# A new list for the even mixer in quarter slices, an earlier first input, earlier bank release and a later spread of the norm's factors in a two-layer encoder trunk

## The chip, the core and the metric

The kernel runs on one core of one Trainium2 chip. The time is the device time of one execution in microseconds (us). Before the change it is 1195.79 us, the median of 3 runs (1194.28 to 1196.98). The core has five engines with a queue of instructions each: PE (matmuls), DVE (vector), ACT (scalar), POOL (GpSimd) and SP, which issues nearly all of the DMAs.

## The reference, cut to what matters

The input is one sequence of 256 tokens of 1024 numbers. Two layers follow one another; each has a SwiGLU feed-forward part (FFN), a mixer, and a second FFN. The mixer of layer 0 ("even") runs attention and a recurrence (RWKV-7) side by side, that of layer 1 ("odd") is a retention.

```
x = x + 0.5 * rms_norm(swiglu(rms_norm(x, g[0]), w_gu, w_d), g[1])
h = rms_norm(x, g[2])
z = h @ w_in                                 # even mixer: q, k, v of attention; r, k, v, low of RWKV-7
oa = rms_norm(diff_attention(qa, ka, va, lam), subln) * (1 - lam_init)
ob = group_norm(rwkv7_recurrence(r, decay, k, v, kk, a)) + bonus, times the gate
x = x + rms_norm(concat(oa, ob) @ w_out, g[3])
x = x + 0.5 * rms_norm(swiglu(rms_norm(x, g[4]), w_gu, w_d), g[5])
```

swiglu(x) is (silu(x W_gate) * (x W_up)) W_down with an inner width of 2816. The recurrence's token shift mixes each token's value with that of the token before it.

## The kernel before

**Tiling.** The 256 tokens are two blocks of 128, b0 and b1 (in the tables x_75 and x_76). All products keep fp32 accuracy by splitting each operand in two parts, a high one (xh, wh) and a rest (xl, wl). A weight tile `raw` (128x1024, 512 KB) is loaded by SP, ACT casts it to `wh` (L307), DVE subtracts to get `wl` (L308). `pump` issues the loads in the order of use and at most so far ahead as there are buffers. A projection of 512 columns is 24 matmuls on two units of weights (L327 to L329), an output product 12 for each unit (L341 to L343), a projection with the weights held still 48 of 256 columns (L354 to L356). The FFN's 11 chunks of 256 inner columns are done for each block apart ("solo") or for both blocks at once ("joint", L370 and L371); JOINT says which. The first FFN has chunk 0 solo, the other three have chunks 0 and 1 solo.

**Norms.** `pre` transposes a block on PE (L434) and writes xp on ACT and DVE (L439, L440). The norm's factor `rs` of a row is a sum of squares on ACT (L421), a sum on DVE (L413) and a power on POOL (L416). Solo chunks take it as a scalar; joint chunks need it along the free axis, so `spread` copies it on DVE to `rw` (L454), transposes that on PE (L456) and copies the result to `rsb` on ACT (L457). `post` (L468 to L487) adds a block's result: two sums of squares on ACT, two products on DVE, a power on POOL, and two updates of x (L487).

**The even mixer.** Its PE order is written by a small planner: a stream of the units in EVEN_ORDER (the two blocks in turn), cut in slices, and between the slices the steps of jobs (feature, low, value, the recurrence's `core`, attention) by their rank, as soon as an estimated clock has reached the time that each step's `yield` gives. The other engines' order follows from priorities. For each block and for each of two groups of 256 columns, `rwkv_features` makes decays (pc L1074, w L1077, L1078), `kk` (L1082), and on POOL the product `fr` (L1095); the sums `pn` (L1109 on kk, L1110 on fr) follow. Then come pl (L1157), px (L1164) and a chain of small products p (L1175, L1181) with DVE steps between. Value (L833 to L840) moves z one token down by DMAs that POOL issues, since b1's first row comes from b0. At the end of the core comes the group norm (L1313 to L1325), and `mr`; attention ends with hx (L1047); four output units of each block follow, first those of attention.

**Buffers.** `t2` is one pool of five tiles for all short-lived rows of 512: z, zs, mu, kk, low, rw, yg, sgh and others.

Of the kernel before, what the change touches and what calls it, by code (L numbers as in the profile page):

```python
# [17 lines left out]
P = 128  # L18
# [10 lines left out]

NRAW0, FIRST = 12, 56  # L30
CONSTANTS = 40
LAG = 3
LAG0 = (6, 12)
WIDE = 16
LIFT_PRE, LIFT_POST = 300, 100
X = (0, 1, 2)
SPLIT = 6
# [6 lines left out]

EVEN_ORDER = ("k", "r", "low", "q2", "k2", "v", "v2")
PLAN = [("ffn", 0, 0), ("even", 0, 0), ("ffn", 0, 1), ("ffn", 1, 0), ("odd", 1, 0), ("ffn", 1, 1)]
# [59 lines left out]
def _layout(inputs):  # L106
# [23 lines left out]
    def even():  # L130
        w, out = a["even_w_in"][0], []
        b0 = 1536
        at = {"k": b0 + 512, "r": b0, "v": b0 + 1024, "q2": 0, "k2": 512, "v2": 1024}
        for c in EVEN_ORDER:
            if c == "low":
                out += list(cols(w[:, b0 + 1536 :], 8))
            elif c in ("q2", "k2"):
                out += [cols(w[:, i : i + 256], 8)[0] for i in (at[c], at[c] + 256)]
            else:
                out += list(cols(w[:, at[c] : at[c] + 512]))  # L140
        return out + list(cols(a["even_w_out"][0], 2))

# [70 lines left out]
class Trunk:  # L213
    def __init__(self, ctx, tc, io, out, plan):
        self.tc, self.nc, self.io, self.out, self.plan = tc, tc.nc, io, out, plan
        nc = self.nc
        pool = lambda *a, **k: ctx.enter_context(tc.tile_pool(*a, **k))
        self.sb = pool(name="sb", bufs=1)
        self.raw_p = pool(name="raw", bufs=NRAW)
        self.w_p = pool(name="wsp", bufs=NW)  # L220
        self.ps_p = pool(name="ps", bufs=2, space=PSUM)
        self.mix = None
        self.even_cm = tc.tile_pool(name="even", bufs=1)
        self.even_p = self.even_cm.__enter__()
        self.first_cm = tc.tile_pool(name="first", bufs=NRAW0)
        self.first_p = self.first_cm.__enter__()

        c0 = self.sb.tile([P, P + PR_N], F32, name="c0")
        self.ident, self.par = c0[:, :P], c0[:, P:]
        self.mhalf = self.sb.tile([P, 8], F32, name="mhalf")  # L230
        self.x = [self.sb.tile([P, D], F32, name=f"x{b}") for b in range(2)]
        nc.sync.dma_start(out=c0, in_=io["c0"])

        self.ahead = {X[0]: [(0, 0)], X[1]: [(0, 1)], X[2]: [(1, 0), (1, 1)]}
        nc.vector.memset(self.mhalf, -0.5)

# [45 lines left out]
    def pump(self):  # L282
# [3 lines left out]
        while self.n_split < lim:  # L286
            while self.n_dma < min(2 * self.n_units, self.n_split + (NRAW0 if self.n_dma < FIRST else NRAW)):
                i = self.n_dma
                for b, q in self.ahead.pop(i, ()):
                    c = slice(q * 512, q * 512 + 512)  # L290
                    nc.sync.dma_start(out=self.x[b][:, c], in_=self.io["x"][b * P : (b + 1) * P, c])
                r = (self.first_p if i < FIRST else self.raw_p).tile([P, 1024], F32, tag="raw", name="raw")
                self.tc.keep_in_program_order(
# [23 lines left out]
    def proj_slices(self, ps, u, first, last, xT, width=512):  # L317
# [5 lines left out]
        for i in range(n):  # L323
# [5 lines left out]
            mm(ps[:, :width], lhsT=xl[:, kt, :], rhs=h[:, c], start=False, stop=last and i == n - 1)  # L329
            if i == n // 2 - 1:  # L330
                yield "slice", 1.4

# [12 lines left out]
    def features_slices(self, ps, u):  # L345
# [3 lines left out]
        for t in range(2):  # L349
            o = ps[:, t * 256 : t * 256 + 256]  # L350
            for kt in range(8):
                h, l = w[kt // 4]
                c = slice(kt % 4 * 256 + t * P, kt % 4 * 256 + t * P + P)
                mm(o, lhsT=h[:, c], rhs=xh[:, kt], start=kt == 0, stop=False)  # L354
                mm(o, lhsT=h[:, c], rhs=xl[:, kt], start=False, stop=False)
                mm(o, lhsT=l[:, c], rhs=xh[:, kt], start=False, stop=kt == 7)  # L356
                if kt == 3 or (kt == 7 and not t):
                    yield "slice", 1.4

# [132 lines left out]
    def ffn(self, b, u, l, j):  # L492
# [14 lines left out]
        for c in range(NCH + 1):  # L507
            if c == 3:
                self.gpost(gi)
            if c < NCH and not c0 <= c < c1:  # L510
# [11 lines left out]
                u += 1  # L522
                if c0 < c1 and b not in J:
                    self.spread(b, rs)
                    J[b] = True
                t = self.t2("sgh")
                sg, h[c] = t[:, :256], t[:, 256:]
                nc.scalar.activation(out=sg, in_=ps[:, :256], func=AF.Silu, scale=rs[:, 0:1])
                nc.vector.tensor_tensor(out=h[c], in0=ps[:, 256:], in1=sg, op=ALU.mult)
                yield  # L530
# [171 lines left out]
    def even(self, b, u, l, j):  # L702
# [57 lines left out]
        def feature(ps, name, mu, om_at):  # L760
            z = scaled(ps, T2("z"))
            yield 0, 1.3
            yield from self.room(2.6)
            tp = transposes(z, 4)
# [107 lines left out]
        for c in EVEN_ORDER:  # L872
            if c in ("q2", "k2"):
                for i in range(2):
                    if b == 0:
                        ps = self.ps("mm")
                        yield from self.features_slices(ps, u)
                        (queries if c == "q2" else keys)(i, ps)
                        self.stream_took = 1.4
                    else:  # L880
                        self.stream_took = 0
                    u += 1
                    if i and c == "k2":
                        att = self.spawn(1 + 3 * b, self.attention(b, S[f"qT{b}"], kT, rs), 1.5)
                    yield
                continue
            ps = self.ps("mm")
            if c != "low":
                yield from self.proj_slices(ps, u, True, False, xT)
                self.stream_took = 1.4  # L890
                u += 1
# [6 lines left out]
            else:  # L898
                yield from self.proj_slices(ps, u, True, True, xT, 256)
            self.stream_took = 1.4  # L900
            u += 1
            if c in jobs:
                job = self.spawn(2 * b, jobs[c](ps))
                if c == "low":
# [12 lines left out]
        acc = None  # L917
        for i, job in enumerate((att, att, core, core)):
            while not job["done"] or self.now < job["at"] or (acc is None and not free()):
                yield "wait"  # L920
            if acc is None:
                acc = [self.ps(("mm", "ac1")[b]) for _ in range(2)]
            self.outp(acc, u, S.pop(f"{'mr' if i > 1 else 'att'}{b}{i % 2}"), i == 0, i == 3)
            self.stream_took = 2.8
# [50 lines left out]
    def attention(self, b, qT, kT, rs):  # L975
# [6 lines left out]
        ss = self.small(4, "ss4", 2)  # L982
        ma = self.hx(b).bitcast(F32).rearrange("p (a t) -> p a t", a=4)
        for h0 in range(0, 4, H):
            heads = range(h0, h0 + H)
# [28 lines left out]
            for i in range(H):  # L1014
# [4 lines left out]
                )  # L1019
            yield 1.7, 8.0  # L1020
            while f"av{b}" not in S or "pT" in S:
# [25 lines left out]
        V.tensor_tensor(out=ma, in0=ma, in1=r4[:, :, None].to_broadcast([P, 4, P]), op=ALU.mult)  # L1047
        yield 0, 5.0
        for i in range(2):
# [328 lines left out]
    def run(self):  # L1378
# [28 lines left out]

        sizes = {"low": 1, "out": 4}
        turns, at = [], next(at for at, kind in bounds.items() if kind == "even")
        for c in EVEN_ORDER + ("out",):  # L1410
            n = sizes.get(c, 2)
# [76 lines left out]
```

## Time and profile before

| | |
|---|---|
| median of 3 runs | 1195.79 us |
| lowest and highest | 1194.28, 1196.98 us |
| the profiled execution | 1200.61 us, of which its span is 1198.8 us |
| busy in the span | PE 96%, DVE 62%, ACT 52%, POOL 4% |
| granted PE clock, mean | 0.986 of full speed |

One execution was recorded. Its rows give start times from the start of the span. An instruction's row shows in square brackets how long its engine had stood idle before it and what ended that. The durations of matmuls overlap (each is longer than the time to the next), so the pitch from start to start is what a matmul costs. The granted clock is the share of full speed that PE had in a stretch. The profiled execution is 4.82 us longer than the median.

### The profile page before, as it was taken

Reading aid. Unit: us, or ns where it says so; the run is one execution under the profiler, and the core shown is the slowest. Engines: PE = TensorE matmul, PEld = TensorE weight load, DVE = VectorE, ACT = ScalarE, POOL = GpSimd, SP = SyncE. Lnnn points to the kernel's source line nnn. Section 1 sums busy time; section 2 is a strip of 40 time slices with the busy share of each in tenths; the row PEclk is TensorE's granted clock in tenths of the full one; section 3 lists DMA queues with packets and bytes.
Section 4 is the critical chain, followed back from the end, with each engine's and each line's share of the span. In section 5 each row is a group of like instructions: output and inputs, shape, how many; then the busy total and the mean of one; then the engine's idle time right before and its main releaser. Section 6 shows DMA issues by size and latency. Waiting matters only on the chain.

```text
span 1198.8 us, 18578 instructions
## 1 busy us (share of the span) xinstructions
PE 1152.4 (96%) x7314; PEld 955.5 (80%) x7314; DVE 744.8 (62%) x1124; ACT 626.2 (52%) x1054; POOL 51.7 (4%) x79
## 2 busy tenths in 40 slices
PE   6999999999999799999999999999999999999997
PEld 5888887788778687888878888877877777888886
DVE  6665667667663656656676666675545557566664
ACT  7554456763242555555565555575434456555552
POOL 0000000012120100000010000010000001000000
PEclk9999999999999899999999999999999999999999
DMA  9766245432320346555646555556534554656551
GB/s 361 278 209 198 89 134 184 144 120 85 115 89 1 122 149 220 179 190 179 206 138 214 195 182 175 194 188 210 176 98 160 172 168 158 209 184 189 191 192 37
DMA packets 55657, 200.26 MB, mean 167 GB/s; under 512 B 6289, under 2 KB 6545, under 8 KB 55569
## 3 DMA queue, kind: packets, MB, share of 16 engines
q1 hardware_dynamic: 54576, 196.45, 49.2%
q0 software_dynamic: 704, 2.10, 0.6%
q8 instruction: 57, 0.93, 0.3%
q10 hardware_dynamic: 288, 0.52, 0.1%
q14 instruction: 32, 0.25, 0.1%
HBM read 197.47 MB, written 1.05 MB: 166 GB/s over the span
## 4 chain that ended last, share of the span: by engine, by line
PE 77%; DMA 8%; DVE 7%; ACT 4%; issue 2%; POOL 1%; SPq 0%; DVEq 0%; POOLq 0%; ACTq 0%
PE ps L370 22%; PE ps L371 11%; PE ps L341 7%; PE ps L343 7%; PE ps L342 7%; DMA raw<-in_wts_dram 7%; PE ps L327 5%; PE ps L329 4%; PE ps L328 4%; DVE wl L308 3%; ACT wh L307 2%; PE yp L619 1%; DMA x<-in_x_dram 1%; PE tp L387 1%; PE tp L434 1%
## 5 line engine op out<-in xcount | busy, mean ns | idle before, releaser
L308 DVE TENSOR_TENSOR wl<-raw,wh 128x1024 fp32r<-128x1024 f32 (+1 forms) x368 | 442.2, 1207 | 258.5 <-ACT wh L307 256.7
L307 ACT CAST wh<-raw 128x1024 fp32r<-128x1024 f32 (+1 forms) x368 | 379.9, 1038 | 240.6 <-PE ps L370 74.1
L370 PE MATMUL ps<-xp,wh 128*128 128x512 f32 x1312 | 467.4, 398 | 5.7 <-DVE gate L380 2.7
L371 PE MATMUL ps<-xp,wl 128*128 128x256 f32 x1312 | 367.7, 280 | 0.0
L370 PEld LDWEIGHTS ps<-xp,wh 128*128 128x128 f32 x1312 | 245.9, 187 | 71.4 <-DVE gate L380 11.5
L371 PEld LDWEIGHTS ps<-xp,wl 128*128 128x128 f32 x1312 | 247.8, 189 | 1.5
L341 PE MATMUL ps<-wh,hx 128*128 128x512 f32 x432 | 173.7, 402 | 0.1
L342 PE MATMUL ps<-wl,hx 128*128 128x512 f32 x432 | 172.2, 399 | 0.0
L343 PE MATMUL ps<-wh,hx 128*128 128x512 f32 x432 | 171.9, 398 | 0.0
L327 PE MATMUL ps<-wh,xp 128*128 128x512 f32 (+1 forms) x320 | 132.4, 416 | 2.0 <-ACT xp L439 1.9
L328 PE MATMUL ps<-wl,xp 128*128 128x512 f32 (+1 forms) x320 | 126.4, 396 | 0.2 <-DVE wl L308 0.2
L329 PE MATMUL ps<-wh,xp 128*128 128x512 f32 (+1 forms) x320 | 125.5, 394 | 1.0 <-DVE xp L440 0.9
L341 PEld LDWEIGHTS ps<-wh,hx 128*128 128x128 f32 x432 | 82.1, 190 | 19.6 <-ACT hx L394 0.5
L343 PEld LDWEIGHTS ps<-wh,hx 128*128 128x128 f32 x432 | 81.9, 190 | 19.8
L342 PEld LDWEIGHTS ps<-wl,hx 128*128 128x128 f32 x432 | 82.2, 190 | 17.6
L327 PEld LDWEIGHTS ps<-wh,xp 128*128 128x128 f32 x320 | 61.2, 191 | 19.6 <-ACT xp L439 5.9
L329 PEld LDWEIGHTS ps<-wh,xp 128*128 128x128 f32 x320 | 61.1, 191 | 16.3 <-DVE xp L440 3.1
L379 ACT COPY gate<-ps 128x256 f32<-128x256 f32 x74 | 27.2, 368 | 88.1 <-PE ps L371 88.1
L328 PEld LDWEIGHTS ps<-wl,xp 128*128 128x128 f32 x320 | 61.6, 192 | 12.9 <-issue 1.9
L380 DVE TENSOR_TENSOR gate<-ps,gate 128x256 f32<-128x256 f32 x74 | 31.1, 421 | 58.1 <-ACT gate L379 58.1
L379 ACT COPY h<-ps 128x256 f32<-128x256 f32 x74 | 27.2, 367 | 50.1 <-PE ps L371 50.0
L440 DVE SCALAR_TENSOR_TENSOR xp<-tp,c,xp 128x128 fp32r<-128x128 f32 x96 | 30.5, 347 | 15.7 <-ACT xp L439 14.7
(269 smaller groups left out, 947.3 us busy)
## 6 DMA issues: line engine op xcount, KB each, us to landing
raw<-in_wts_dram SPq DMA_DIRECT2D x362, 512.0 KB, 4.6
gpost<-in_rows_dram SPq DMA_DIRECT2D x6, 512.0 KB, 6.1
x<-in_x_dram SPq DMA_DIRECT2D x4, 256.0 KB, 6.8
ups<-in_ups_dram SPq DMA_DIRECT2D x1, 768.0 KB, 6.4
mu<-in_rows_dram POOLq DMA_DIRECT2D x2, 256.0 KB, 4.0
lnw<-in_rows_dram POOLq DMA_DIRECT2D x2, 256.0 KB, 4.9
lnb<-in_rows_dram POOLq DMA_DIRECT2D x2, 256.0 KB, 5.4
dec<-in_co_dram SPq DMA_DIRECT2D x1, 512.0 KB, 7.2
```

Source lines behind the costliest of these rows:

```text
L307: nc.scalar.copy(out=h[:, c], in_=r[:, c])
L308: nc.vector.tensor_tensor(out=l[:, c], in0=r[:, c], in1=h[:, c].bitcast(F32), op=ALU.subtract)
L327: mm(ps[:, :width], lhsT=xh[:, kt, :], rhs=h[:, c], start=first and i == 0, stop=False)
L328: mm(ps[:, :width], lhsT=xh[:, kt, :], rhs=l[:, c], start=False, stop=False)
L329: mm(ps[:, :width], lhsT=xl[:, kt, :], rhs=h[:, c], start=False, stop=last and i == n - 1)
L341: mm(acc[n], lhsT=hh[:, t], rhs=wh[:, c], start=first and t == 0, stop=False)
L342: mm(acc[n], lhsT=hh[:, t], rhs=wl[:, c], start=False, stop=False)
L343: mm(acc[n], lhsT=hl[:, t], rhs=wh[:, c], start=False, stop=last and t == 1)
L370: mm(ps, lhsT=h[:, c], rhs=both, start=kt == 0, stop=False)
L371: mm(ps[:, :256], lhsT=l[:, c], rhs=both[:, :256], start=False, stop=kt == 7)
L379: self.nc.scalar.copy(out=o, in_=ps[:, 256:])
L380: self.nc.vector.tensor_tensor(out=o, in0=ps[:, :256], in1=o, op=ALU.add)
```

## The change

There are five edits, in the order of the program.

- **Start.** SP loads both halves of b0 before the first weight tile, and b1 after the second tile (X). The pool of twelve buffers that serves the first weight tiles now begins at tile 6; tiles 0 to 5 take the three buffers of the ordinary pool (FIRST).
- **Solo chunks.** silu and the product behind it get a higher priority (LIFT_OUT), so that their banks are read before other work of ACT and DVE.
- **Spread.** It is made in the last solo chunk before the joint ones: a chunk later in the three FFNs that have two.
- **The mixer's list.** EVEN_ORDER puts value ahead of q2 and k2. Slices are a quarter of a unit. The two groups of attention's scores are both made before the first is used. The ranks are b for core and 2 + b for attention. The output units take the core's result first, then attention's, and the blocks take turns two units at a time. Second values (v2) wait until b1's features are formed.
- **Estimates.** Three of the planner's numbers (2.6 to 3.6; 8.0 to 0.5 and 7.5; 5.0 to 6.5).

```diff
-NRAW0, FIRST = 12, 56
+NRAW0, FIRST = 12, (6, 56)
-LIFT_PRE, LIFT_POST = 300, 100
-X = (0, 1, 2)
+LIFT_PRE, LIFT_POST, LIFT_OUT = 300, 100, 200
+X = (0, 2)
-EVEN_ORDER = ("k", "r", "low", "q2", "k2", "v", "v2")
+EVEN_ORDER = ("k", "r", "low", "v", "q2", "k2", "v2")
-        self.ahead = {X[0]: [(0, 0)], X[1]: [(0, 1)], X[2]: [(1, 0), (1, 1)]}
+        self.ahead = {X[b]: [(b, 0), (b, 1)] for b in range(2)}
...
-            if i == n // 2 - 1:
-                yield "slice", 1.4
+            if i % (n // 4) == n // 4 - 1 and i < n - 1:
+                yield "slice", 0.7
...
-                if c0 < c1 and b not in J:
+                if c0 < c1 and b not in J and c == c0 - 1:
                     self.spread(b, rs)
                     J[b] = True
                 t = self.t2("sgh")
                 sg, h[c] = t[:, :256], t[:, 256:]
-                nc.scalar.activation(out=sg, in_=ps[:, :256], func=AF.Silu, scale=rs[:, 0:1])
-                nc.vector.tensor_tensor(out=h[c], in0=ps[:, 256:], in1=sg, op=ALU.mult)
+                with self.tc.high_priority(LIFT_OUT):
+                    nc.scalar.activation(out=sg, in_=ps[:, :256], func=AF.Silu, scale=rs[:, 0:1])
+                    nc.vector.tensor_tensor(out=h[c], in0=ps[:, 256:], in1=sg, op=ALU.mult)
...
-                        att = self.spawn(1 + 3 * b, self.attention(b, S[f"qT{b}"], kT, rs), 1.5)
+                        att = self.spawn(2 + b, self.attention(b, S[f"qT{b}"], kT, rs), 1.5)
...
+            while c == "v2" and "formed1" not in S:
+                yield "wait"
...
-                job = self.spawn(2 * b, jobs[c](ps))
+                job = self.spawn(b, jobs[c](ps))
...
-        for i, job in enumerate((att, att, core, core)):
+        for i, job in enumerate((core, core, att, att)):
```

The loads of the start on SP, where b0 is x_75 and b1 is x_76. Before:

```order
L291 DMA x_75<-in_x_dram 128x512
L294 DMA raw<-in_wts_dram 128x1024
L291 DMA x_75<-in_x_dram 128x512
L294 DMA raw<-in_wts_dram 128x1024
L291 DMA x_76<-in_x_dram 128x512 x2
L294 DMA raw<-in_wts_dram 128x1024 x31
```

The same of the kernel after, with what each load waits for:

```order
L292 DMA x_75<-in_x_dram 128x512 x2
L295 DMA raw<-in_wts_dram 128x1024 x2
L292 DMA x_76<-in_x_dram 128x512 x2
L295 DMA raw<-in_wts_dram 128x1024
L295 DMA raw<-in_wts_dram 128x1024 [waits DMAHW3_49,DMAHW0_49,DVE_49]
L295 DMA raw<-in_wts_dram 128x1024 [waits DMAHW1_49,DMAHW4_49,DVE_49,Activation_49]
L295 DMA raw<-in_wts_dram 128x1024 [waits DMAHW7_49,DMAHW2_49,DVE_49]
```

The second half of b0 moved ahead of the first weight tile, b1 behind the second, and the fourth to sixth tiles now wait for ACT's and DVE's work on the first three.

POOL's queue in the mixer, from the features on: fr is the product of `rwkv_features`, mu, zs and ups belong to value. Before:

```order
L1095 TENSOR_TENSOR fr<-fr,ta 128x256 x4
L1252 MEMSET work 128x512
L1205 COPY inv_2521<-work 32x8x32 x4
L1192 COPY work<-work 32x8x32
L1200 COPY work<-work 32x8x32
L271 DMA mu<-in_rows_dram 128x512
L833 DMA zs<-z 127x512
L838 DMA ups<-z 1x16x32
L271 DMA mu<-in_rows_dram 128x512
L833 DMA zs<-z 127x512
L835 DMA zs<-ups 1x16x32
```

After:

```order
L272 DMA mu<-in_rows_dram 128x512
L835 DMA zs<-z 127x512
L840 DMA ups<-z 1x16x32
L1104 TENSOR_TENSOR fr<-fr,ta 128x256
L272 DMA mu<-in_rows_dram 128x512
L835 DMA zs<-z 127x512
L837 DMA zs<-ups 1x16x32
L1104 TENSOR_TENSOR fr<-fr,ta 128x256
```

The first block's two products stood at the head of this queue; now three DMA issues stand ahead of each.

PE at the end of the mixer, from b1's last products (py, pg) on; L387 transposes hx of attention and work of the core. Before:

```order
L1302 MATMUL py<-work,gram 128x64
L1324 MATMUL pg<-ups,sxg 128x512
L387 MATMUL tp<-c_73,hx 128x128 x4
L341 MATMUL ps<-wh,hx 128x512
L342 MATMUL ps<-wl,hx 128x512
```

After, first at the same place, where a projection's slices now stand:

```order
L1311 MATMUL py<-work,gram 128x64
L1333 MATMUL pg<-ups,sxg 128x512
L1046 MATMUL op<-av,pT 128x128 x4
L328 MATMUL ps<-wh,xp 128x512
L329 MATMUL ps<-wl,xp 128x512
```

and further down, where the core's second half of b1 is transposed:

```order
L343 MATMUL ps<-wl,mr 128x512
L344 MATMUL ps<-wh,mr 128x512
L388 MATMUL tp<-c_73,work 128x128 x2
L388 MATMUL tp<-c_73,hx 128x128 x2
L1046 MATMUL op<-av,pT 128x128 x4
L1038 MATMUL tp<-c_73,s 128x128 x4
L342 MATMUL ps<-wh,mr 128x512
```

Eighteen matmuls of projection, twelve of output and the last steps of b1's attention moved behind b1's pg; before, the next matmul after pg was the transpose of hx.

## Rows read from the trace of the kernel before

**Rows 1.** The page's head: busy time of the engines, and the chain that ended last.
```profile
PE 1152.4 (96%) x7314; PEld 955.5 (80%) x7314; DVE 744.8 (62%) x1124; ACT 626.2 (52%) x1054; POOL 51.7 (4%) x79
...
PE 77%; DMA 8%; DVE 7%; ACT 4%; issue 2%; POOL 1%; SPq 0%; DVEq 0%; POOLq 0%; ACTq 0%
```

**Rows 2.** PE's waits: line, what it waited for, total us, times, longest.
```profile
PE tp L434 <- DMA x<-in_x_dram: 7.3, 2, 3.8
PE tp L387 <- DVE hx L1047: 6.4, 1, 6.4
...
PE tp L456 <- DVE rw L454: 2.6, 2, 2.1
PE tp L787 <- DVE fr L751: 2.1, 1, 2.1
...
PE p L1175 <- DVE work L1183: 1.9, 1, 1.9
...
PE ps L370 <- DVE sgh L529: 1.5, 1, 1.5
```

**Rows 3.** Stretches: length, busy of PE, PEld, DVE, ACT, POOL; clock, DMA, GB/s.
```profile
30.00:190.00 160.00, 160.00 (x840) 135.52 (x839) 102.66 (x135) 83.50 (x118) 2.58 (x7) 1.00 0.53 180
...
300.00:385.00 85.00, 79.74 (x1129) 67.27 (x1129) 48.32 (x87) 29.72 (x71) 13.38 (x19) 0.96 0.22 71
385.00:411.00 26.00, 19.48 (x91) 15.55 (x91) 15.76 (x28) 11.31 (x26) 2.64 (x2) 0.80 0.20 65
```

**Rows 4.** ACT at the start of the kernel, in order of time.
```profile
9.58 0.37 ACT L439 ACTIVATE xp<-tp,c 128x128 fp32r<-128x128 f32 x1 [2.18 <-PE tp L434]
...
20.91 2.03 ACT L307 CAST wh<-raw 128x1024 fp32r<-128x1024 f32 x2
22.80 0.30 ACT L457 COPY rsb<-tp 128x128 f32<-128x128 f32 x1
23.11 1.28 ACT L528 ACT_TABLE_LOAD   x1
24.41 0.48 ACT L528 ACTIVATE sgh<-ps,rs 128x256 f32<-128x256 f32 x1
```

**Rows 5.** The page's DMA issues: engine, form, count, KB each, us to landing.
```profile
raw<-in_wts_dram SPq DMA_DIRECT2D x362, 512.0 KB, 4.6
```

**Rows 6.** POOL in the mixer: the products fr, and value's DMA issues.
```profile
255.18 0.75 POOL L1095 TENSOR_TENSOR fr<-fr,ta 128x256 f32<-128x256 f32 x1 [1.74 <-DVE ends L1097]
258.50 2.87 POOL L1095 TENSOR_TENSOR fr<-fr,ta 128x256 f32<-128x256 f32 x1 [2.57 <-DVE ends L1097]
...
298.17 0.57 POOL L833 DMA_DIRECT2D zs<-z  x1 [1.37 <-ACT z L715]
298.73 0.52 POOL L838 DMA_DIRECT2D ups<-z  x1
```

**Rows 7.** DVE beside the second product fr.
```profile
258.42 2.35 DVE L308 TENSOR_TENSOR wl<-raw,wh 128x1024 fp32r<-128x1024 f32 x2
```

**Rows 8.** PE at the mixer's end, before the output products of b1.
```profile
387.24 1.08 PE L1324 MATMUL pg<-ups,sxg 128*128 128x512 f32 x2
394.70 1.09 PE L387 MATMUL tp<-c,hx 128*128 128x128 f32 x4 [6.38 <-DVE hx L1047]
...
410.30 0.39 PE L343 MATMUL ps<-wh,mr 128*128 128x512 f32 x1
410.53 0.39 PE L327 MATMUL ps<-wh,xp 128*128 128x512 f32 x1
```

**Rows 9.** DVE in the same place: the group norm's first and last step.
```profile
387.85 0.69 DVE L1313 TENSOR_REDUCE mean<-work 128x8 f32<-128x512 f32 x1 [2.21 <-ACT work L1303]
...
396.74 0.68 DVE L1325 TENSOR_TENSOR work<-pg,work 128x512 f32<-128x512 f32 x1
```

**Rows 10.** Stretches of 5 us around the wait at the mixer's end and the next.
```profile
395.00:400.00 5.00, 4.86 (x14) 3.60 (x13) 2.36 (x5) 0.90 (x2) 0.00 (x0) 0.50 0.00 0
...
420.00:425.00 5.00, 5.00 (x20) 4.18 (x21) 1.74 (x6) 2.06 (x7) 0.13 (x1) 0.66 0.33 103
```

**Rows 11.** DVE: b1's last update of x at the mixer's end.
```profile
416.38 1.41 DVE L487 SCALAR_TENSOR_TENSOR x<-yg,rsp,x 128x512 f32<-128x512 f32 x2
```

More of the change, by code (lines that the diff above doesn't have):

```diff
@@ L140, in even @@
                 out += list(cols(w[:, at[c] : at[c] + 512]))
-        return out + list(cols(a["even_w_out"][0], 2))
+        wo = list(cols(a["even_w_out"][0], 2))
+        return out + wo[2:] + wo[:2]
     def odd():
@@ L286, in pump @@
         while self.n_split < lim:
-            while self.n_dma < min(2 * self.n_units, self.n_split + (NRAW0 if self.n_dma < FIRST else NRAW)):
+            while self.n_dma < min(2 * self.n_units, self.n_split + (NRAW0 if FIRST[0] <= self.n_dma < FIRST[1] else NRAW)):
                 i = self.n_dma
@@ L291, in pump @@
                     nc.sync.dma_start(out=self.x[b][:, c], in_=self.io["x"][b * P : (b + 1) * P, c])
-                r = (self.first_p if i < FIRST else self.raw_p).tile([P, 1024], F32, tag="raw", name="raw")
+                r = (self.first_p if FIRST[0] <= i < FIRST[1] else self.raw_p).tile([P, 1024], F32, tag="raw", name="raw")
                 self.tc.keep_in_program_order(
@@ L356, in features_slices @@
                 mm(o, lhsT=l[:, c], rhs=xh[:, kt], start=False, stop=kt == 7)
-                if kt == 3 or (kt == 7 and not t):
-                    yield "slice", 1.4
+                if kt % 2 and (kt < 7 or not t):
+                    yield "slice", 0.7
     def proj_parts(self, u, t):
@@ L762, in feature @@
             yield 0, 1.3
-            yield from self.room(2.6)
+            yield from self.room(3.6)
             tp = transposes(z, 4)
@@ L878, in even @@
                         (queries if c == "q2" else keys)(i, ps)
-                        self.stream_took = 1.4
+                        self.stream_took = 0.7
                     else:
@@ L889, in even @@
                 yield from self.proj_slices(ps, u, True, False, xT)
-                self.stream_took = 1.4
+                self.stream_took = 0.7
                 u += 1
@@ L899, in even @@
                 yield from self.proj_slices(ps, u, True, True, xT, 256)
-            self.stream_took = 1.4
+            self.stream_took = 0.7
             u += 1
             if c in jobs:
-                job = self.spawn(2 * b, jobs[c](ps))
+                job = self.spawn(b, jobs[c](ps))
                 if c == "low":
@@ L922, in even @@
                 acc = [self.ps(("mm", "ac1")[b]) for _ in range(2)]
-            self.outp(acc, u, S.pop(f"{'mr' if i > 1 else 'att'}{b}{i % 2}"), i == 0, i == 3)
+            self.outp(acc, u, S.pop(f"{'att' if i > 1 else 'mr'}{b}{i % 2}"), i == 0, i == 3)
             self.stream_took = 2.8
@@ L983, in attention @@
         ma = self.hx(b).bitcast(F32).rearrange("p (a t) -> p a t", a=4)
+        probs = []
         for h0 in range(0, 4, H):
@@ L1019, in attention @@
                 )
-            yield 1.7, 8.0
+            probs.append((heads, s))
+            yield 1.7, 0.5
+        yield 0, 7.5
+        for heads, s in probs:
+            h0 = heads[0]
             while f"av{b}" not in S or "pT" in S:
@@ L1047, in attention @@
         V.tensor_tensor(out=ma, in0=ma, in1=r4[:, :, None].to_broadcast([P, 4, P]), op=ALU.mult)
-        yield 0, 5.0
+        yield 0, 6.5
         for i in range(2):
@@ L1406, in ready @@
             return ahead < lag
-        sizes = {"low": 1, "out": 4}
+        sizes = {"low": 1}
         turns, at = [], next(at for at, kind in bounds.items() if kind == "even")
-        for c in EVEN_ORDER + ("out",):
+        for c in EVEN_ORDER + ("out", "out"):
             n = sizes.get(c, 2)
```

## The prediction

> **What bounds the kernel now.** I read the page's head first: PE is busy 96% of the span and carries 77% of the chain that ended last [rows 1]. So only two things count: what PE waits for, and how fast it is clocked. The stretches give the place. From 30 to 190 us (the first FFN) PE is busy 160.00 of 160 us at full clock, and no edit can gain there. From 385 to 411 us, the mixer's end, it is busy 19.48 of 26 us at a granted clock of 0.80 [rows 3]. Then I read PE's waits by length: 7.3 us for the first input in two waits, 6.4 us for hx of b1's attention at the mixer's end, 2.6 us for the spread's rw, of which one wait is 2.1, 2.1 for low, 1.9 in the recurrence's chain, 1.5 for silu before the joint chunks [rows 2]. A wait also costs behind itself: after the 6.4 us wait PE ran at 0.50 from 395 to 400 us [rows 10], half of full speed (1.2 instead of 2.4 GHz), which is 2.5 us of work lost, and after the rw wait at 0.66 from 420 to 425 us [rows 10], 0.34 of 5 us or 1.7 us. I price a new wait of about 3 us or more at its length plus 1.7.
>
> **The start.** ACT stands idle 2.18 us before the second half of b0's transposes reach it [rows 4], because that half is loaded behind a weight tile. The new order loads it ahead of it. The first weight tile comes half a b0 later in exchange, about half of what one weight tile takes, so I count 0.9 us of the 2.18. ACT is then the bound until the joint chunk: before it, silu ran at 24.41 us, behind two casts (2.03), the copy of rsb (0.30) and a table load (1.28) [rows 4], while PE waited 1.5 us [rows 2]. With LIFT_OUT the silu goes ahead of the casts. The casts are still needed by the joint chunk, so I take 1.1 of the 1.5 us. Sum: -2.0. The lower end is both whole, 2.18 + 1.5, -3.7. The upper end comes from the new wait in SP's queue: tile 3 can only be issued when tile 0 is split, and behind it stand all later tiles. A tile's load lands 4.6 us after its issue [rows 5]. If tiles 3 to 5 each come a fraction of that too late, the gain is gone and 1 us with it: +1.
>
> The Trainium skill, page "SBUF — State Buffer", section "The DMA setup-cost knee", says that every transfer pays a fixed cost of about 2 us, whatever its size; loads issued one by one show it, queued ones hide it. By the page's fit 512 KB take 3.2 us (an estimate), against the 4.6 us of the rows, and the start would come out between -2.0 and +1. It speaks against the three tiles that now wait.
>
> **The spread.** In the second FFN rw is copied late, because rs waits for x of b1, written from 416.38 us on [rows 11], and PE stands 2.1 us at L456, then loses 1.7 us of clock [rows 2, 10]. A chunk later, 24 matmuls of projection and 12 or more of output lie between; at 0.23 us each (410.30 to 410.53 [rows 8]) that is over 8 us of cover, and the wait of 2.1 us fits in it four times. What is late next there is silu of the solo chunk, which is lifted. So -3.8 us. The other half microsecond of rw waits (2.6 - 2.1) goes too: -0.5. Bounds: 0 if the same wait comes back at silu, -4.3.
>
> **The mixer, what goes.** Between b1's pg at 387.24 and the transpose of hx at 394.70 PE had nothing to do, because attention's last step was late behind the group norm's chain on DVE [rows 8, 9]. In the new order 18 matmuls of projection, 12 of output and attention's steps lie behind pg. So the 6.4 us go and the 2.5 us of clock behind them: -8.9. From 300 to 385 us PE is busy 79.74 of 85 us [rows 3], 5.3 us of small waits, and 1.9 us lie in the chain ahead of that [rows 2]; the finer slices fill such gaps. I take all of this, -7.2, as gone, and let the new waits stand for what comes back. The clock of 0.96 over these 85 us [rows 3] is 3.4 us lost, which goes with the waits: -3.4. Sum: -19.5. The wait for low (2.1) has the same order around it and stays.
>
> **The mixer, what comes.** I walked the new order with the durations of before.
>
> (a) Value now comes ahead of q2, and so its DMA issues stand in POOL's queue ahead of the products fr of b0. fr of the second group stands behind b1's zs, which waits for z of b1, the product of the matmuls just ahead of pn on PE. So pn cannot follow them: it waits for z on ACT, two issues on POOL (0.57 and 0.52) and fr, which took 0.75 us once and 2.87 us the other time [rows 6]. z is a pass over 512 columns, which takes DVE 0.69 [rows 9]; I take the same for ACT. Together 2.5 to 4.7 us; hand-overs add, pn's first half takes off, and I let these two cancel. I take 3.8. The clock's dip adds 1.7. The 2.87 us product ran beside a DVE subtraction of two inputs in SBUF, from 258.42 on for 2.35 us [rows 7]; in the new order such subtractions stand here too, which is why I take the upper half.
>
> The Trainium skill, page "SBUF — State Buffer", section "SBUF: two separate sides", has this as a rule: a GpSimd operation that reads SBUF and a DVE operation with two inputs in SBUF shut each other out for a whole instruction. These two rows agree. By the rule alone the term would be 4.7 + 1.7 whenever a wl is running, 0.9 more than I take.
>
> (b) px behind it waits for DVE, where one of value's passes (0.69 [rows 9]) and one wl (half of 2.35 [rows 7]) stand ahead: 1.9, say 2 us. (c) Attention's scores of b0 need the keys' product, which DVE makes behind a wl and a pass of b0's norm: 1.2 + 2 x 0.69, 2.6 us. (d) The group norm of b1 takes from 387.85 to 396.74 plus 0.68 [rows 9], 9.6 us, and the copies ahead of and the transposes behind it some 2 more, against 18 + 12 matmuls and three small steps of cover, 30 x 0.23 + 1.3 = 8.2 us: 3.4 us of wait, plus 1.7 of clock. (e) The next FFN's transposes of b0 follow its last output product after only 9 matmuls and one transpose (2.5 us), while post took from 410.5, the end of b1's output, to 417.8 in before [rows 8, 11]. Part of that was queueing; I take 5.5 against 2.5, 3 us, and 1.7 of clock. (f) b0's chain has fewer projection matmuls to fill it: half of the old 1.9 us again, 1.0 us.
>
> Sum of (a) to (f): 5.5 + 2 + 2.6 + 5.1 + 4.7 + 1.0 = 20.9. So the mixer comes out at -19.5 + 20.9 = +1.4. Bounds: with (a) covered, (c) and (e) at nothing, -11; with (a), (d) and (e) each 3 us larger, +10.
>
> **What costs nothing.** Quarter slices change no matmul, only where others may cut in. The exchanged output units are the same 96 matmuls. PE is not granted less for it.
>
> **Sum.** -2.0 - 4.3 + 1.4 = -4.9 us. The profiled execution of before took 1200.61, so 1195.7; it lay 4.82 above the median, so the prediction is 1190.9, in round numbers **1191.0** us.
>
> **Rivals.** *Everything in the mixer is covered:* the new walk's waits shrink because planner and queues have slack I don't see. The mixer is then -11, the sum -17.3, about 1178.5. For it: 6.4 and 2.5 us go for certain. Against it: (a) and (d) are waits for chains whose lengths stand in rows. *POOL's queue makes b0 late (slower):* fr behind b1's zs holds pn, pn holds all of b0's chain, and with fewer fill matmuls each of its links shows as a wait; the mixer is then +10, the sum +3.7, about 1199.5. It decides from a mixer loss of 6.3 us, the sum of the other two gains. For it: fr at 2.87 us and no projection left between pn and px. Against it: the chain's links in before waited just 1.9 us in all. *The change does not do what it says at the start and at the spread:* tiles 3 to 5 eat the first gain, the silu of the second FFN takes the place of rw, and the mixer nets nothing: -1 to +1, about 1195.5.
>
> **Chances.** Forecast (1184 to 1193.4) 0.45, all covered 0.15, no change 0.15, slower 0.25. About 0.2% is what a measurement of this kernel can tell from no change, 2.4 us. So faster 0.60, same 0.15, slower 0.25. The range must leave out no more than 2 in 10: it goes from 1180 (most of the covered case) to 1200 (the slower case with its price of +10 in the mixer).
>
> **What would show it.** First S512 and joint chunk: silu at 20.5 to 23.5 instead of 24.41 us [rows 4], and PE's wait of 1.5 for it shorter. The rw wait of 2.1 gone and 420 to 425 at full clock. No idle after pg. New: a wait of L1119 for fr on POOL of 3 to 5 us near 260; a wait of L388 for work of the core of 2 to 5 us; one of L435 for x of b0 of 1 to 5 us. The second FFN's first matmul near 411. I am wrong if pn waits for nothing, if the second FFN starts before 404, or if it starts after 416.

## The result, and the profile after

The change made the kernel slower: a median of 1208.69 us (1205.38 to 1210.05, 4 runs) against 1196.38 us of before, measured beside it. The ratio is 1.0101, with a 95% interval of 1.0075 to 1.0126. I had forecast 1191.0 us, so the sign was wrong as well as the size.

The profiled execution of after is the shortest of its four, 1205.38 us with a span of 1203.6 us, which is 4.8 us longer than before's span. The other three had a lower mean granted clock (0.979 to 0.981 against 0.986); where the clock goes is told below. The profile shows where the time went, stage by stage. Lines are moved by 1 or 2, in the mixer by up to 9 (L1095 is L1104 now, L1175 is L1184, L1181 is L1190).

| stage (first matmul of the next stage ends it) | before | after | difference |
|---|---|---|---|
| start, to the first joint chunk | 25.43 | 25.93 | +0.5 |
| first FFN, to the mixer's first projection | 176.93 | 176.64 | -0.3 |
| mixer, to the second FFN's first projection | 208.17 | 220.08 | +11.9 |
| all that follows | 788.27 | 780.95 | -7.3 |

The page's PE waits of after, in the form of [rows 2]:

```profile
PE tp L435 <- DMA x<-in_x_dram: 4.0, 1, 4.0
PE ps L328 <- ACT wh L308: 3.8, 1, 3.8
PE p L1190 <- issue: 3.0, 2, 2.0
PE tp L388 <- DVE work L1334: 3.0, 1, 3.0
PE p L1206 <- issue: 2.9, 1, 2.9
...
PE sp L999 <- DVE akT L851: 2.5, 1, 2.5
PE tp L388 <- DVE hx L1056: 1.9, 1, 1.9
...
PE pn L1119 <- POOL fr L1104: 1.5, 1, 1.5
PE pn L1118 <- ACT kk L1107: 1.3, 1, 1.3
...
PE pn L1118 <- issue: 0.7, 1, 0.7
```

The 6.4 us at the mixer's end and the 2.1 us of rw are gone, as forecast. The second FFN starts at 422.65 us, later than the 416 us that I had named as a sign of being wrong. New is a kind of wait that is not in the list of before: "issue", a gap in which PE waited for nothing that the profile shows. Five such gaps, 7.0 us in sum, lie between 275 and 306 us, four of them (6.3 us) in the recurrence's bursts of small products and one (0.7) among the sums pn. This is the largest, in the order of time:

```profile
301.90 0.59 PE L1206 MATMUL p<-work 32*32 32x32 f32 x26
305.42 0.22 PE L1206 MATMUL p<-work 32*32 32x32 f32 x2 [2.92 <-issue]
```

PE stops in the middle of a burst whose products all read the same two tiles, so it is no tile that came late. The other thing to read is the clock, in stretches of 5 us of after (columns as in [rows 3]):

```profile
255.00:260.00 5.00, 3.44 (x20) 2.85 (x18) 5.00 (x15) 4.80 (x9) 1.61 (x3) 1.00 0.39 118
260.00:265.00 5.00, 3.77 (x40) 3.04 (x41) 3.45 (x7) 0.94 (x3) 1.43 (x3) 0.64 0.67 199
265.00:270.00 5.00, 4.89 (x79) 3.98 (x78) 4.36 (x10) 3.19 (x8) 1.70 (x3) 0.50 0.48 141
270.00:275.00 5.00, 5.00 (x141) 4.59 (x140) 3.05 (x10) 1.26 (x4) 0.00 (x0) 0.84 0.82 230
...
305.00:310.00 5.00, 4.58 (x107) 4.12 (x107) 1.48 (x4) 2.56 (x7) 0.00 (x0) 0.57 0.02 3
310.00:315.00 5.00, 5.00 (x96) 4.70 (x97) 1.59 (x3) 0.58 (x1) 0.00 (x0) 0.74 0.36 108
```

After the waits of pn near 260 us, PE ran at half of full speed (1.2 GHz) from 261.4 to 271.6 us, and after the 2.92 us gap from 305.7 to 312.5 us. The work lost is half of these times, 5.0 and 3.4 us. In before the loss behind 6.4 us of idleness was 2.5 us in the stretch of [rows 10], and 2.9 us up to its end at 400.6 us. The clock did not fall behind every gap: from 293 to 305 us, with gaps of 1.06 and 0.37 us, PE kept full speed.

To compare mixers I cut them in stretches of 1 us and summed two things for PE: idle time (1 - busy), and work lost to the clock (busy x (1 - clock)). Between 202 us and the second FFN, before has 20.3 us idle and 11.0 us lost; after has 27.4 and 14.8. That is 10.9 of the 11.9 us. The matmuls are the same, 7314 in both; the last 1.0 us I can't place.

### The profile page after: what moved, and what is told of

Its sections match the earlier page's. It is cut to its first block, busy times and chain, and to the rows that moved or that the text cites. A ratio compares the mean times of both kernels' runs of the same rounds, so it can differ in the third digit from the quotient of the medians.

```text
span 1203.6 us, 18600 instructions
## 1 busy us (share of the span) xinstructions
PE 1155.4 (96%) x7314; PEld 960.1 (80%) x7314; DVE 746.1 (62%) x1124; ACT 627.3 (52%) x1054; POOL 51.3 (4%) x79
## 4 chain that ended last, share of the span: by engine, by line
PE 82%; DVE 6%; DMA 4%; ACT 4%; issue 3%; POOL 1%; SPq 0%; DVEq 0%; POOLq 0%; ACTq 0%
PE ps L371 24%; PE ps L372 12%; PE ps L344 8%; PE ps L343 8%; PE ps L342 8%; DMA raw<-in_wts_dram 4%; PE ps L328 4%; PE ps L330 4%; PE ps L329 4%; DVE wl L309 3%; ACT wh L308 2%; PE ps L355 1%; PE yp L621 1%; PE ps L356 1%; PE ps L357 1%
## 5 line engine op out<-in xcount | busy, mean ns | idle before, releaser
L342 PE MATMUL ps<-wh,hx 128*128 128x512 f32 x432 | 171.0, 396 | 0.8 <-ACT hx L395 0.8
L344 PE MATMUL ps<-wh,hx 128*128 128x512 f32 x432 | 170.8, 395 | 0.0
L342 PEld LDWEIGHTS ps<-wh,hx 128*128 128x128 f32 x432 | 81.1, 188 | 20.3 <-ACT hx L395 1.0
L417 POOL TENSOR_TENSOR rsp<-ssv,mhalf 128x1 f32<-128x1 f32 x12 | 11.0, 920 | 645.8 <-DVE ssv L414 645.8
```

The costliest lines, as they stand in the source:

```text
L342: mm(acc[n], lhsT=hh[:, t], rhs=wh[:, c], start=first and t == 0, stop=False)
L344: mm(acc[n], lhsT=hl[:, t], rhs=wh[:, c], start=False, stop=last and t == 1)
```

## The experiments

The theory at this point: with quarter slices, fewer large matmuls lie between two bursts of small products, and PE uses up its instructions faster than they arrive (theory one). The rival is my own step: value's place in POOL's queue ahead of fr (theory two). The runs of before beside the experiments had medians from 1196.3 to 1198.5 us, so ratios are compared, not times.

| run | what it is | ratio to before | 95% interval |
|---|---|---|---|
| e1 | no mixer part: start, silu, spread | 0.9977 | 0.9954 to 0.9999 |
| e2 | start alone | 0.9995 | 0.9975 to 1.0016 |
| e14 | silu and spread alone | 0.9979 | 0.9955 to 1.0004 |
| e3 | after with half slices | 1.0051 | 1.0031 to 1.0071 |
| e4 | after with value late in the list | 1.0111 | 1.0084 to 1.0138 |
| e5 | before with quarter slices | 1.0126 | 1.0084 to 1.0168 |
| e6 | before, small products twice | 1.0194 | 1.0146 to 1.0242 |
| e9 | after, half as many instructions in 16 bursts | 0.9951 | 0.9928 to 0.9974 |
| e10 | before, half as many instructions in 16 bursts | 0.9971 | 0.9953 to 0.9990 |
| e7 | after, half slices, output order of before | 1.0068 | 1.0041 to 1.0096 |
| e8 | after, half slices, ranks of before | 1.0105 | 1.0064 to 1.0145 |
| e13 | after, half slices, value late | 1.0107 | 1.0073 to 1.0141 |
| e11 | e1 with value early | 1.0078 | 1.0051 to 1.0105 |
| e12 | e1 with both scores first | 1.0003 | 0.9983 to 1.0023 |
| e15 | e1 with the new output order | 1.0073 | 1.0046 to 1.0100 |

### Outside the mixer: e1, e2, e14

e1 undoes every edit of the mixer. e2 undoes these, the lifted silu and the spread, and so keeps the first two lines below; e14 keeps the other part.

```diff
+NRAW0, FIRST = 12, (6, 56)
+X = (0, 2)
...
+                if c0 < c1 and b not in J and c == c0 - 1:
+                with self.tc.high_priority(LIFT_OUT):
```

> The new start, the lifted silu and the later spread alone; the mixer (list, slices, ranks, scores, output order, estimates) as before. In the two profiles the stretch from the second FFN's first matmul to the end is 7.3 us shorter after the change (788.27 against 780.95 us) and the start 0.2 us longer. If these parts stand by themselves, the kernel is 5 to 7 us faster than before (about 1190), without the 2.1 us wait for rw and with a clock of 1.00 after it. If the gain behind the mixer hangs on the mixer's new end (which block's x comes first, which tiles are loaded by then), it is 0 to 3 us.

> Before, with the new start alone (inputs ahead of weight tile 0, tiles 0 to 5 from three buffers). The profile after the change shows no gain there: the wait of 3.5 us for x becomes one of 3.8 us for the cast of the first tile. Expected: the same as before within 1 us, with waits of 4.0 for x and 3.8 for wh L308. A rival: without the lifted silu the joint chunk's wait of 1.5 us stays and the three tiles that wait make it 1 to 2 us slower.

> Before, with the lifted silu and the later spread alone, without the new start and the mixer. The profile of before loses 2.1 us of wait and 1.7 us of clock there. If these two parts are the whole gain of the kernel without the mixer's part (0.9977), this one is at 0.996 to 0.998 as well; if the new start has a share in it, at 0.998 to 1.000.

e1 is faster than before by 0.23%, some 2.8 us. That is half of the larger gain that I had named (5 to 7 us) and inside the smaller one (0 to 3 us); the interval just leaves out no change. e14 has the same ratio without the start, and e2, the start alone, is not to be told from before. So silu and spread carry the gain, as far as 0.2% can be split at all. e1's stretch behind the mixer's end has no rw wait and full clock, where before had 0.66 [rows 10]:

```profile
420.00:425.00 5.00, 5.00 (x25) 4.06 (x24) 3.12 (x5) 3.06 (x6) 0.00 (x0) 1.00 0.12 16
```

### Which of the two theories: e3, e4, e5

e3 is after with the old slices (the same in the projection with the weights held still, and 1.4 for the stream's step). e4 is after with the old list. e5 is before with the quarter slices and nothing else.

```diff
-            if i % (n // 4) == n // 4 - 1 and i < n - 1:
-                yield "slice", 0.7
+            if i == n // 2 - 1:
+                yield "slice", 1.4
...
-EVEN_ORDER = ("k", "r", "low", "v", "q2", "k2", "v2")
+EVEN_ORDER = ("k", "r", "low", "q2", "k2", "v", "v2")
```

> After, with slices of half a unit as before. Theory one: PE's own instructions run out where bursts of small matmuls stand close together (waits put down to issue, 7.0 us between 275 and 306 us, each followed by the lower clock): with 12 instead of 6 matmuls between bursts these waits shrink to under 2 us and the mixer gets 6 to 12 us shorter, 1197 to 1203. Theory two: the mixer's loss is value's place in POOL's queue ahead of fr: then it stays at 1205 to 1210 and the waits of pn stay at 3 us or more.

> After, with value behind the keys' second part as before (and without the wait of the second values for the features). Theory two (value's DMA issues stand ahead of fr on POOL): the 3.5 us of waits at pn and the half clock behind them (5 us) go, 6 to 9 us faster than after, 1199 to 1203. Theory one (PE's instructions run out): the waits put down to issue stay and pn's gain is in part given back, 1203 to 1207.

> Before, with slices of a quarter unit alone. Half slices in the kernel after took away nearly all waits put down to issue and 5.1 us. If quarter slices alone bring bursts of small matmuls too close together for the supply of PE's instructions, waits put down to issue of 2 to 7 us appear here too and the kernel is 3 to 8 us slower than before. If they do so only together with the ranks that interleave both blocks' chains, there are under 1 us of them and the time is within 3 us of before.

e3 takes back half of the loss, and its waits put down to issue fall from 7.0 to 0.6 us; pn waits for nothing. But other waits came (6.8 us for work at the mixer's end, 4.6 for inv): by the sums above its mixer has 28.3 us idle, no less than after, and 7.9 us lost to the clock. So e3 alone doesn't decide. e4 also removes pn's waits, and the time stays where it was: 1.0111. It doesn't decide either, since it gets a new wait, the one below. e5 shows that quarter slices alone cost about as much as the whole change (1.26% and 1.01%, with intervals that overlap). Its longest wait in the mixer, with the old list:

```profile
PE pr L1264 <- DVE rv L842: 9.2, 2, 4.8
```

In e5 a job's step comes after every 6 large matmuls of 256 columns instead of 12, so the recurrence runs ahead of the stream of projections and gets to pr before value (rv) has been projected. e4 has the same wait (9.3 us). Before and e13, which have the old list with half slices, don't have this wait, and after, with value early, doesn't either. So with quarter slices value has to come early, and undoing its place alone (e4) gains nothing. Of issue waits e5 has only 2.8 us, 2 to 7 expected, and by the sums above 19.7 us lost to the clock; the size of its loss was missed (3 to 8 us expected, about 15 measured).

### PE's instructions: e6, e9, e10

e6 writes the 32 products p1 and the 32 products p2 of each of the recurrence's rounds twice, to the same place. e9 and e10 write 16 products of 64 columns instead of 32 of 32, in after and in before; they use one head's factor for two heads, so every second head's part is left out. In the rows a product in fp32 is two records.

```diff
-            for h in range(8):
+            for h in [h for _ in range(2) for h in range(8)]:
...
-            for h in range(8):
+            for h in range(0, 8, 2):
                 for q in range(4):
-                    mm(p1[Q[q], h], lhsT=nt[Q[q], h, Q[q % 2]], rhs=xx[Q[q], h], start=True, stop=True)
+                    mm(p1[Q[q], h : h + 2], lhsT=nt[Q[q], h, Q[q % 2]], rhs=xx[Q[q], h : h + 2], start=True, stop=True)
```

> Before, with each of the 16 bursts of 32 small products (p1 and p2 of the recurrence, written twice to the same place) doubled; nothing else is changed, the result is the same. A burst takes 0.68 us of PE in the profile of before, so 16 x 0.68 = 10.9 us more if only PE's time counts, and no waits put down to issue. If the supply of PE's instructions is a limit, the doubled bursts stop in the middle: waits put down to issue, some 1 to 2.5 us each, 10 to 30 us in sum, each ending 2 to 3 us after a packet of the instruction queue.

> After, with the recurrence's 16 bursts of 32 products of 32 columns written as 16 products of 64 columns: the same columns, half of the instructions (it uses one head's factor for two heads, so every second head's part is left out of the computation). If the supply of PE's instructions is what stops PE, the 7.0 us of waits put down to issue go below 2 us and the half clock behind them (some 6 us in that profile) goes too: 8 to 14 us faster than after, less what the control gains. If the waits put down to issue have another cause (banks, weights), they stay and the gain is that of the control.

> The control: before, with the same 16 bursts of half as many products of double width (again every second head's part is left out). Before has no waits put down to issue. At 0.68 us a burst and at most half of it saved, 16 x 0.34 = 5.4 us at the most; as the chain waits for DVE in many places, 0 to 4 us faster than before.

e6 lost 1.94%, some 21 us more at the median of the runs (its profiled execution was longer), against 10.9 us if only PE's time counted. Before has no issue waits to speak of; here they are the largest group of all:

```profile
PE p L1181 <- issue: 6.5, 5, 3.0
...
PE p L1175 <- issue: 4.1, 3, 2.1
```

One of them, in time, again in the middle of a burst:

```profile
295.82 0.26 PE L1181 MATMUL p<-work 32*32 32x32 f32 x9
299.09 0.45 PE L1181 MATMUL p<-work 32*32 32x32 f32 x31 [3.01 <-issue]
```

What may end such a gap can be seen among the DMAs. The page lists a queue of its own for instructions, the same in before and after: 57 packets, 0.93 MB, so 16 KB each.

```profile
q8 instruction: 57, 0.93, 0.3%
```

That it brings PE's instructions can be seen from the runs that changed their number. e6 has 8338 matmul records instead of 7314, e9 and e10 have 6802, each with as many weight loads, and the queue follows:

```profile
q8 instruction: 65, 1.06, 0.3%
...
q8 instruction: 53, 0.87, 0.3%
```

2048 instructions more are 8 packets more, 1024 fewer are 4 fewer: one packet for 256 instructions of PE, by these counts.

In after I looked for these packets in stretches of half a microsecond: in those that begin at 274.5, 285.5, 293.0, 296.5 and 303.0 us there is one each, and PE goes on at 276.97, 288.18, 295.80, 299.18 and 305.42 us, 2.4 to 2.8 us behind the stretch's start each time. In e6 one lies in the stretch from 296.5 us, and PE goes on at 299.09. Packets at 279.0, 289.0, 306.5 and 311.0 us in after have no such gap behind them, so a packet alone doesn't stop PE. This is what was read off, not a test.

The test is e9. Its bursts take as long as those of after: 32 records in 0.65 us, where after has 62 records in 0.71 us (the burst at 301.34 us).

```profile
288.77 0.65 PE L1184 MATMUL p<-work 32*32 32x64 f32 x32
```

With half of the instructions and the same time on PE in a burst, no issue wait is left in the list, and the whole change comes out at 0.9951 of before; the control e10 is at 0.9971. So with the short bursts' supply out of the way, the change would be at 0.9951 / 0.9971 = 0.998 of its control, the side that I had forecast, with intervals that overlap. The same change with the full number of instructions is at 1.0101. e9 gained more on after than I had expected (1.5%, some 18 us, against 8 to 14). By the sums above its mixer has 18.9 us idle and 13.4 lost to the clock, after's 27.4 and 14.8: what went is idle time, mostly the issue gaps, and hardly any of the clock's loss.

e9 also answers theory two. It keeps value's place, both waits of pn and the half clock behind them (260.4 to 274.0 us), and isn't slow:

```profile
PE pn L1119 <- POOL fr L1104: 1.5, 1, 1.5
...
PE pn L1118 <- ACT kk L1107: 1.3, 1, 1.3
...
265.00:270.00 5.00, 4.89 (x76) 3.44 (x75) 3.92 (x10) 2.31 (x6) 1.42 (x3) 0.50 0.35 123
```

So value's place in POOL's queue, which I had given the largest single price, isn't enough to make after slow. Whether it is free isn't shown: in the profiles e9's mixer, with all of its edits, takes 208.4 us and its control's 203.0, with 13.4 against 7.8 us lost to the clock. (These are single executions, e9's 1.4 us above its median and e10's 2.5 below.) And 0.998 is no more than silu and spread give alone (0.9979 in e14). Even with half of the instructions, then, nothing here shows a gain of the mixer.

I take it as shown that the number of PE instructions in the bursts, in the order that quarter slices give, is what turned the change from no loss into a loss of 1%. That the missing instructions come through the packets above is what the times suggest; no run held the packets back by itself.

### What half slices leave: e7, e8, e11, e12, e13, e15

e3 is still 0.5% behind before and 0.7% behind e1. These runs undo one part more of e3 (e7: output order, e8: ranks, e13: list) or add one part to e1 (e11: list, e12: scores, e15: output order).

```diff
-        for i, job in enumerate((core, core, att, att)):
+        for i, job in enumerate((att, att, core, core)):
...
-                        att = self.spawn(2 + b, self.attention(b, S[f"qT{b}"], kT, rs), 1.5)
+                        att = self.spawn(1 + 3 * b, self.attention(b, S[f"qT{b}"], kT, rs), 1.5)
...
-            probs.append((heads, s))
-            yield 1.7, 0.5
-        yield 0, 7.5
-        for heads, s in probs:
-            h0 = heads[0]
+            yield 1.7, 8.0
```

> After, with half slices and with the output units as before (attention first, four of a block in a row). With half slices alone the longest wait is 6.8 us for the core's last product (work of b1), as the core's units stand first in the output. If that order costs the rest, the wait goes down to 2 to 4 us and the kernel is at 1196 to 1200, with no loss against before. If not, another wait of 6 us (hx, as before) takes its place and it stays at 1202 to 1205.

> After, with half slices and the ranks of before (b0's core, b0's attention, b1's core, b1's attention). If the interleaved chains of both blocks cost the rest (4.6 us of wait for inv, 2 us for st), these go below 2 us and the kernel is at 1197 to 1200. If not, 1202 to 1206.

> After, with half slices and value at its old place in the list; ranks, scores, output order and estimates as after. Value's early place alone cost about 1% (1.0078 against 0.9977 without it). If that and the slices are all of the loss, this kernel is at 0.995 to 1.000 of before. If ranks or output order cost as well, 1.003 to 1.008.

> Start, lifted silu and spread as after, and of the mixer only the new place of value in the list and the wait of the second values for the features; half slices and all else as before. Without the new list this kernel ran at 0.9977 of before. If value's early place (POOL's queue ahead of fr, other filling of the recurrence) costs what is left of the loss with half slices (0.5 + 0.2 to 0.3%), it is at 1.004 to 1.008 of before. If not, 0.996 to 1.001.

> Start, lifted silu and spread as after, and of the mixer only both groups of attention's scores ahead of their use. If that costs the rest, 1.004 to 1.008 of before with a longer wait at the mixer's end than 6.4 us; if it is neutral, 0.996 to 1.000.

> Start, lifted silu and spread as after, and of the mixer the output order alone (the core's units first, the blocks in turn two at a time). If the core's group norm at the mixer's end now shows where attention's wait of 6.4 us was: a wait for work or hx of 5 to 7 us and 0.997 to 1.001. If the units between cover it: under 3 us there and 0.992 to 0.996.

None of the three undone parts brings e3 back to before; e13 is worse than e3, and e8 too by its median (the intervals just touch). Added alone to e1, value's early place costs 1.0% and the output order 1.0%, more than all of them together in e3. The scores cost nothing that can be told (e1's interval overlaps). So the parts don't add up, and the remaining 0.5 to 0.7% can't be put on one of them. This stays open.

What e11 and e15 lose is to be seen, though, and it is mostly the clock. By the sums used above, to the second FFN, e1 has 19.6 us idle and 8.9 us lost to the clock; e11 has 24.4 and 18.9, e15 24.2 and 19.6. e15 in the last part of the recurrence:

```profile
375.00:380.00 5.00, 4.32 (x21) 4.32 (x22) 1.64 (x6) 2.08 (x8) 0.00 (x0) 0.59 0.00 0
380.00:385.00 5.00, 4.50 (x25) 3.67 (x24) 2.17 (x4) 1.64 (x4) 0.00 (x0) 0.50 0.00 0
385.00:390.00 5.00, 4.82 (x23) 4.82 (x23) 0.00 (x0) 1.13 (x6) 0.00 (x0) 0.50 0.00 0
390.00:395.00 5.00, 4.08 (x13) 2.50 (x12) 1.55 (x3) 0.96 (x2) 0.00 (x0) 0.50 0.00 0
395.00:400.00 5.00, 0.46 (x3) 0.49 (x4) 2.92 (x6) 0.04 (x1) 2.62 (x2) 0.50 0.00 2
400.00:405.00 5.00, 3.19 (x11) 2.13 (x11) 3.05 (x6) 1.64 (x4) 0.00 (x0) 0.50 0.01 3
405.00:410.00 5.00, 5.00 (x20) 4.06 (x19) 1.59 (x2) 2.00 (x2) 0.00 (x0) 0.83 0.00 0
```

and before, in its last part:

```profile
370.00:375.00 5.00, 5.00 (x46) 4.54 (x46) 1.73 (x3) 0.00 (x0) 0.00 (x0) 1.00 0.00 0
375.00:380.00 5.00, 5.00 (x34) 4.48 (x34) 3.20 (x7) 2.59 (x11) 0.00 (x0) 1.00 0.01 2
380.00:385.00 5.00, 3.96 (x36) 3.33 (x36) 4.71 (x9) 2.51 (x8) 1.81 (x2) 1.00 0.00 0
```

Before has two groups of 12 output products of 512 columns among these small products (at 368 and 375 us). In e15 these come after the recurrence, and a wait of 2.3 us before py (for gram, on DVE) is followed by 30 us at half clock, through small products and the waits at the end, until output products run. e11 has the like behind 3.1 us for gram, at half clock from 388 to 412 us. As I read these traces, the products that fill the recurrence are not only worth the idle time that they cover; they were also what PE did while its clock stayed up. No run put these two groups back by themselves, so this is argued, not shown.

## Why the prediction was wrong

**What costs nothing** is the step that failed first. I wrote that quarter slices change no matmul, only where others may cut in, and gave them no price. Alone they cost 1.26% (e5). They change two things that I left out: how fast the jobs advance against the stream (the 9.2 us for rv in e5), and how close bursts of small products come (7.0 us of issue gaps in after, none listed in before). In the whole change the second is what counts: with half of the instructions in the bursts it is at 0.998 of its control (e9, e10), with all of them the change is at 1.0101 of before.

**The mixer, what comes: the clock.** This is the second step that failed. I priced each dip at 1.7 us, read from the one behind rw [rows 10]. Behind pn it was half speed from 261.4 to 271.6 us, 5 us, and behind the last issue gap 3.4 us. The short dips of before, behind waits of 0.8 to 2.1 us, all had products of the projections or the output in them; behind pn none of these ran up to 268.67 us. My dips came to 5.1 us new against 5.9 gone, -0.8 in sum; measured were +3.8 in the shortest run of after.

**The mixer, what comes: the waits.** Without the issue gaps, idle time in the mixer is the same in both profiles (27.4 - 7.0 against 20.3), and my sum was 15.8 against 13.6, +2.2. By item: (a) pn waited 2.8 us, 3.8 forecast, but 1.3 of it for kk on ACT; fr took 1.13 us, between my two rows, though a wl ran beside its first 0.55 us. (b) px waited for nothing, 2 forecast. (c) the scores waited 2.5 for akT, 2.6 forecast. (d) the transposes at the end waited 1.9 + 3.0, 3.4 forecast. (e) the next FFN's transposes of b0 didn't wait for x; hx of b1 cost 0.8 there, 3.0 forecast. (f) 0.6 for work, 1.0 forecast. So the walk of the order with the durations of before was right to about 2 us an item, and of no use for the sign, since what it didn't contain was larger.

**The mixer, what goes.** The 6.4 us at the end went, but not the idle time as a whole: hx and work wait there for 4.8 us.

```profile
391.29 0.44 PE L388 MATMUL tp<-c,hx 128*128 128x128 f32 x2 [1.85 <-DVE hx L1056]
394.71 0.66 PE L388 MATMUL tp<-c,work 128*128 128x128 f32 x2 [2.98 <-DVE work L1334]
```

**The start** was mis-sized: -2.0 forecast, +0.5 measured, and e2 can't be told from no change. Of the 2.18 us I counted 0.9 as gained, so some 1.3 us as the price of the first tile's later place; no row gave that split. ACT casts that tile at 9.04 us now, 2.5 us later than the 6.52 us of before:

```profile
9.04 0.62 ACT L308 CAST wh<-raw 128x512 fp32r<-128x512 f32 x1 [2.73 <-DMA raw<-in_wts_dram]
```

PE's second wait for x (3.5 us in before) became a wait of 3.8 us for wh. The upper bound that I had given for the three tiles that wait holds. SP issues the first two of them at 11.53 and 13.91 us, the third at 17.86, where before had issued 11 tiles between 4.22 and 15.08 us:

```profile
11.53 0.33 SPq L295 DMA_DIRECT2D raw<-in_wts_dram  x1
13.91 0.33 SPq L295 DMA_DIRECT2D raw<-in_wts_dram  x1
```

PE waits for none of the three: between the wait for wh and the joint chunk it waits only 0.7 us, for rw. In all it is idle for 8.5 us up to there, against 9.1 in before. Why the start isn't shorter for that stays open.

(The Trainium skill's fixed cost per transfer, page "SBUF — State Buffer", section "The DMA setup-cost knee", spoke against this, with a result between -2.0 and +1. The +0.5 lies there; no run separated the fixed cost from the tiles' waits. That queued loads hide that cost isn't in this section. The rows agree that loads overlap: 180 GB/s [rows 3] are, as an estimate, one tile in about 2.9 us, and a tile lands 4.6 us after its issue [rows 5].)

**The spread** was right: the 2.1 us wait and the half clock behind it are gone, and silu takes no time in their place. The profile's last stage gives more than the 4.3 us, 7.3, but part of that can be the execution, as before's was 4.8 us above its median. e14's median says less, 0.21% or 2.5 us, with an interval from 0.45% to nothing.

**The rivals.** The slower one had the right sign and, at 1199.5 us, not the size. Its mechanism, POOL's queue, held pn for 2.8 us and cost a dip of 5 us, but wasn't what made the change slow: e9 has both and is no slower than its control. Its second half, that fewer large matmuls between the links of b0's chain would show, was nearer: they showed as issue gaps, not as waits for the links.

## What to carry to other kernels

That finer slices add no work doesn't make them free. Before making the steps between bursts of small matmuls shorter, count PE's instructions in a stretch of some microseconds; PE can run dry in the middle of a burst, and "issue" among its waits says so. Large matmuls that fill a chain of small ones are best kept to its end, as e11 and e15 suggest, and a wait should be priced by what runs behind it: where projection or output products followed at once, half clock lasted 3.4 us in before, where they came late, 10 us in after and 30 us in e15. The short dips in the trace of before were no measure for the second kind.

## What I had not expected of the hardware

Two things. PE's gaps in mid-burst: 0.4 to 2.9 us in after, up to 3.0 us with twice the products (e6), none when each burst had half the instructions (e9). And the length of the slower clock: 3.4 us of time behind the rw wait in before, but 10 us behind pn in after, where small products followed, and 30 us at the mixer's end in e15, where small products and further waits did. The shortest and the longest differ by a factor of nine with waits of like length (2.1 and 2.3 us) ahead of them.
